# Token forms of the product-saving FFN units made in two portions, and S5 input loads split over two DMA queues

## The chip, the cores and the metric

The kernel runs on one core of a Trainium2 chip. The metric is the device time of one execution in microseconds (us); the median of a few runs is compared. Five engines work side by side, each through its own queue of instructions in a fixed order: TensorE (PE, the matmuls; PEld are its weight loads), VectorE (DVE), ScalarE (ACT), GpSimd (POOL) and SyncE (SP, which here only issues DMAs). ACT and POOL can issue DMAs too; such an instruction then stands in that engine's own queue.

## The reference, cut to what matters

The reference is one inference step of a two-layer decoder trunk for 512 prompt tokens and 8 sample tokens, all in float32. Layer 0 mixes with GLA and RG-LRU, layer 1 with S5 and HGRN2; each layer ends in a SwiGLU FFN. Two places matter here:

```python
def swiglu(h, w_in, w_out):
    gate, up = jnp.split(jnp.einsum('bld,df->blf', h, w_in), 2, axis=-1)
    return jnp.einsum('blf,fd->bld', jax.nn.silu(gate) * up, w_out)
...
    u, q, f, i, g = split_cols(z, ODD_SPLITS)
    y, s_re_new, s_im_new = s5_ssm(u, s_re, s_im, lam_re, lam_im, log_dt, b_re, b_im,
                                   c_re, c_im, d_skip)
```

## The kernel before, in words

Activations lie with the features on the partitions: a tile is 128 x 8 x 2 x 260, that is 8 groups of 128 features (index k) and two halves (hf) of 256 prompt and 4 sample tokens. A float32 product is made from three float32r products: each operand is split into a high part (`hhi`, a cast by ACT) and a low part (`hlo`, the rest, a subtraction by DVE), and high x high, low x high and high x low are added (`mm3`, L277 to L288). Weights are loaded as float32 by SP (`raw`, 3 buffers) and split in the same way (`whi`/`wlo`, 3 pairs, L242 to L243; `wxh`/`wxl` are more such tiles). One unit is 128 output features for all tokens: 48 matmuls.

`first_units` (L870) runs the first five units of a stage half by half, so that they can begin when the layer norm has done the first token half. A unit's result stands in `acc` (PSUM, two buffers) until an engine has taken it out: for a gate unit ACT (`sg`, Silu), for an up unit DVE (L1002, `sg` = acc x sg), followed by the split into `ah`/`al`.

**The FFN of layer 1** (`ffn`, L885): its first half (hb = 0) has 12 plain units (`fins`; the first five through `first_units`, L1010, the other seven in the loop at L1011), and then five units through `sw_unit` (L934). Such a unit makes a gate and an up block together from 2 x 2 blocks of weights and tokens with 7 block products in place of 8 (84 matmuls in place of 96). It needs sums of weight blocks (made by DVE in `raw`, L171 to L174) and four sums of token blocks, the token forms t1 to t4, which `t_forms` (L899) makes once. With b11, b12 the lower feature groups (k = 0 to 3) of the two token halves and b21, b22 the upper ones: t1 = b12 - b11, t2 = b22 - t1, t4 = b21 - t2 and t3 = b22 - b12. `join` adds high and low part again (DVE), `parts` splits a form (a cast by ACT, a subtraction by DVE); both go over two k at a time (128 x 520 elements). t1, t2 and t4 have tiles of their own. t3 is written over b12 in `hhi`/`hlo`, so it must wait until no plain unit reads these any more. The temporaries q1, q2, q3 come from the tag `t2k` with 6 buffers, as do `sg` and `p5`. In the program text the call stands behind all 12 plain units, at high priority (L1021 to L1022).

**The S5 input** (`odd_mixer`, L1802): the first four units of the layer-1 input projection make u. Each is written to DRAM (`Ud`, L1830, by SP; the sample tokens to `Usd`, L1850) and read back with another layout into `u8` (L1851 to L1854): eight loads of 128 KB each in rows of 256 bytes, and two small ones with rows of 32 bytes (L1853 into columns 0 to 7, L1854 into columns 73 to 80). All ten are issued by SP in that order. `s5_in` (L1861) multiplies columns 0 to 71 of `u8` (L1871). The trace shows `u8` as `u`.

What sets the order: the program text gives each instruction a place and a priority (`high_priority(offset=...)` moves it ahead by that much), and a planner, with durations that it assumes, then writes the queue of every engine. On the chip each engine takes its queue strictly in that order and waits where an input isn't there yet.

Of the kernel before, what the change touches and what calls it, by code (L numbers as in the profile page):

```python
# [33 lines left out]
HIGH = 3000  # L34
# [6 lines left out]
def build(tc, I, O):  # L41
    nc = tc.nc
    V, S, G, T, SY = nc.vector, nc.scalar, nc.gpsimd, nc.tensor, nc.sync
    with ExitStack() as ctx:
# [19 lines left out]
        def acc_tile():  # L64
            return ps["A"].tile([128, 2, 512], F32, tag="acc", name="acc")
# [4 lines left out]
        def t2k(nm):  # L70
            return tmp.tile([128, 2, HN], F32, tag="t2k", name=nm)
# [41 lines left out]
        def add(out, a, b):  # L113
            tt(out, a, b, ALU.add)
# [38 lines left out]
        LO, UP = slice(0, 4), slice(4, 8)  # L153
# [195 lines left out]
        h = (lambda k: hhi[:, k], lambda k: hlo[:, k])  # L349
# [74 lines left out]
        with tc.tile_pool(name="st", bufs=1, reuse_waits="tile") as st:  # L424
# [34 lines left out]
            for nm, ap in (  # L459
# [12 lines left out]
                n = ap.shape[0]  # L472
# [388 lines left out]
        def mmh(outs, wl_, a, ks, hf):  # L861
            ah, al = a
            ks = list(ks)
            for n, k in enumerate(ks):
                for out, (wh, wl) in zip(outs, wl_):
                    T.matmul(out, wh[:, k, :], ah(k)[:, hf, :], start=n == 0, stop=False)  # L866
                    T.matmul(out, wl[:, k, :], ah(k)[:, hf, :], start=False, stop=False)  # L867
                    T.matmul(out, wh[:, k, :], al(k)[:, hf, :], start=False, stop=n == len(ks) - 1)  # L868

        def first_units(us, alloc):  # L870
            ws.mark((3, 4), alloc)
            ws.off = FIRST
            wsl = [w() for w, _ in us]
            ws.off = HIGH
            for hf in range(2):
                for i in range(0, len(us), 2):
                    acc = acc_tile()
                    pair = list(enumerate(us))[i:i + 2]
                    mmh([acc[:, n - i, :HN] for n, _ in pair], [wsl[n] for n, _ in pair], h, range(8), hf)
                    for n, (_, ev) in pair:  # L880
                        ev(acc[:, n - i:n - i + 1, :HN], slice(hf, hf + 1))
# [3 lines left out]
        def ffn(l, mid=None):  # L885
            with tc.tile_pool(name=f"ff{l}", bufs=1, reuse_waits="tile") as fp:
# [8 lines left out]
                tf = []  # L895
# [3 lines left out]
                def t_forms():  # L899
                    swp = swx.enter_context(tc.tile_pool(name="sw", bufs=1, reuse_waits="tile"))  # L900
                    t1, t2, t4 = [tuple(swp.tile([128, 4, HN], F32R, name=f"t{n}{c}") for c in "hl") for n in (1, 2, 4)]
                    bq = lambda kq, hf: (hhi[:, kq, hf], hlo[:, kq, hf])

                    def join(out, kq, hf):
                        a_, b_ = bq(kq, hf)
                        add(out, a_.bitcast(F32), b_.bitcast(F32))

                    def parts(t, ks, src):
                        S.copy(t[0][:, ks], src)
                        sub(t[1][:, ks], src, t[0][:, ks].bitcast(F32))  # L910

                    t3 = bq(LO, 1)
                    qs = [(slice(q, q + 2), slice(q + 4, q + 6)) for q in (0, 2)]
                    for lo, up in qs:
                        q1, q2, q3 = t2k("q1"), t2k("q2"), t2k("q3")
                        join(q3, lo, 1)
                        join(q1, lo, 0)
                        sub(q1, q3, q1)
                        parts(t1, lo, q1)
                        join(q2, up, 1)  # L920
                        sub(q2, q2, q1)
                        parts(t2, lo, q2)
                        join(q3, up, 0)
                        sub(q3, q3, q2)
                        parts(t4, lo, q3)
                    for lo, up in qs:
                        q2, q3 = t2k("q2"), t2k("q3")
                        join(q3, lo, 1)
                        join(q2, up, 1)
                        sub(q2, q2, q3)  # L930
                        parts(t3, lo, q2)
                    return t1, t2, t3, t4, bq(LO, 0), bq(UP, 0), bq(UP, 1)

                def sw_unit(f):  # L934
                    w1, w2, wu, wg = ws.get("sw", 128 * f)
# [43 lines left out]
                for hb in range(2):  # L979
                    f0 = 11 * hb  # L980
                    fins = []
                    for d in range(0, 11, 2):
                        if l and f0 + d >= SW0:
                            break
                        nj = min(2, 11 - d)
                        fins += [(0, d, j) for j in range(nj)] + [(1, d, j) for j in range(nj)]
                    sg = {}

                    def fin_w(up, d, j):
                        return ws.get("fin", DFF * up + 128 * (f0 + d), 0, j)  # L990

                    def fin_ev(up, d, j, acc, hs=BOTH):
                        m = d + j
                        if up == 0:
                            if hs.start == 0:
                                sg[m] = t2k("sg")
                            act(sg[m][:, hs], acc, AF.Silu)
                            if hb == 0 and hs.stop == 2 and 3 <= m <= 10:
                                affine(last["act"], [m - 3])
                        else:  # L1000
                            s_ = sg[m][:, hs]
                            mul(s_, acc, s_)  # L1002
                            split(ah[:, m, hs], al[:, m, hs], s_)
                            if hs.stop == 2:
                                sg.pop(m)

                    n0 = 0
                    if hb == 0:
                        n0 = 5
                        first_units([(lambda u=u: fin_w(*u), lambda acc, hs, u=u: fin_ev(*u, acc, hs)) for u in fins[:n0]], walloc)  # L1010
                    for u in fins[n0:]:  # L1011
                        w = fin_w(*u)
                        acc = acc_tile()
                        mm3(acc, w, h, range(8))
                        fin_ev(*u, acc[:, :, :HN])
                        if hb == 0 and mid is not None:
                            side = side or mid(fp)
                            next(side, None)
                    if l:
                        if hb == 0:  # L1020
                            with tc.high_priority(offset=HIGH):  # L1021
                                tf[:] = t_forms()  # L1022
                        pg.close()
                        with tc.tile_pool(name=f"pS{hb}", bufs=8, space=PSUM, reuse_waits="tile") as ps["S"]:
                            for f in range(max(SW0, f0), f0 + 11):
                                sw_unit(f)
                        pg.enter_context(psum(2, 4, f"g{hb}"))
                        if hb:
                            swx.close()
                    for _ in side or ():  # L1030
                        pass
                    if hb == 0:
                        gt1 = gate1(l, 5)
                    for mp in range(4 - 2 * hb):
                        accs = [acc_tile() for _ in range(2)]
                        for n, (k0, nk) in enumerate(((8, 3), (0, 8))):
                            for j in range(2):
                                w = ws.get("fout", 256 * mp, f0 + k0, j)
                                mm3(accs[j], w, a, range(k0, k0 + nk), n == 0, n == 1, koff=k0)
                        for j in range(2):  # L1040
                            m = 2 * mp + j
                            if hb == 0:
                                evac_a(m, accs[j], gt1)
                            else:
                                evac_y(m, accs[j], gt1)
# [756 lines left out]
        def odd_mixer():  # L1802
            with tc.tile_pool(name="od", bufs=1, reuse_waits="tile") as mp_:
# [9 lines left out]
                Ud = dr.tile([4, 128, 8, 64], F32, name="Ud")  # L1813
                Usd = dr.tile([4, 128, 8], F32, name="Usd")
                Yd = dr.tile([4, 128, 8, 64], F32, name="Yd")
                Ysd = dr.tile([4, 128, 8], F32, name="Ysd")
                u8 = mp_.tile([128, 32, 81], F32, tag="m10", name="u8", bufs=2)
# [29 lines left out]
                with after_ln():  # L1847
                    G.memset(u8, 0.0)
                    G.memset(X[:, :, 0:1], 0.0)
                SY.dma_start(Usd.rearrange("m p b -> p m b"), u_s)  # L1850
                for e in range(8):  # L1851
                    SY.dma_start(u8[e * 16:(e + 1) * 16, :, 8:72], Ud[:, :, 7 - e, :].rearrange("m (g h) n -> h (m g) n", h=16))
                SY.dma_start(u8[0:16, :, 0:8], Usd.rearrange("m (g h) b -> h (m g) b", h=16))  # L1853
                SY.dma_start(u8[112:128, :, 73:81], Usd.rearrange("m (g h) b -> h (m g) b", h=16))  # L1854

                rot, vr = m8t("rot", (2, 16, 64)), m8t("vr", (2, 16, 64))
# [317 lines left out]
```

## Time and profile before

| | us |
|---|---|
| three runs | 1386.72, 1392.66, 1393.13; median 1392.66 |
| the profiled execution | 1392.64 |
| its span, first to last instruction | 1390.9 |
| around the span | 1.74 |
| busy: PE, DVE, ACT, POOL | 1320.2, 866.3, 551.6, 191.4 |
| mean granted TensorE clock | 0.975 of full speed |

A row of the timeline has start, duration, engine, line, operation, output<-inputs, shape, count and, in brackets, the idle time of the engine before it with what ended it. A row of a windows view has a stretch, its length, the busy time of each engine with its instructions, the granted TensorE clock, the share of the DMA engines that was busy, and GB/s. Line L111 is a helper (every DVE add, subtract and multiply), so tiles tell there what is meant. Times are from the span's start.

### The profile page before, as it was taken

The page shows a single profiled execution, that of the slowest core. Times are in us where ns is not written, and L with a number is a line of the kernel's source. Part 1 is how long each engine was busy: PE and PEld are TensorE (multiplying, and loading weights), DVE is VectorE, ACT ScalarE, POOL GpSimd, SP SyncE. Part 2 cuts the span into 40 slices and gives each one's busy share as a digit, 9 for nine tenths or more (in the row PEclk, how much of TensorE's full clock was granted, in tenths as well). Part 3 has the DMA queues.
Part 4 walks back from the last instruction along what each step waited for, and adds up shares of the span by engine and source line. Part 5 has one row for each costly group of instructions (what it writes and reads, how often), then busy time and mean ns, then how long its engine had stood idle before and what let it go on. Part 6 is the DMA issues. An engine that isn't in the chain of part 4 may idle for free. (4 is left out here: it accounts for less than half of the span.)

```text
span 1390.9 us, 29577 instructions
## 1 busy us (share of the span) xinstructions
PE 1320.2 (95%) x12503; PEld 1252.0 (90%) x12503; DVE 866.3 (62%) x1946; ACT 551.6 (40%) x962; POOL 191.4 (14%) x215
## 2 busy tenths in 40 slices
PE   6899999999999999999998999999897999999996
PEld 4798988999998999998988989889897999999996
DVE  4777755787996233323592784476839743888565
ACT  3554535362333222222264223363534632565431
POOL 2200010340011100000160431013500000000013
PEclk9999999999999999999999999999998999999997
DMA  9633353423446743446458445532121234332311
GB/s 284 210 132 104 111 188 122 152 69 99 137 161 207 241 153 131 145 134 220 149 204 180 136 132 176 145 123 80 61 91 57 77 95 122 92 91 73 126 62 62
DMA packets 172190, 185.53 MB, mean 133 GB/s; under 512 B 18412, under 2 KB 151914, under 8 KB 171802
## 3 DMA queue, kind: packets, MB, share of 16 engines
q1 hardware_dynamic: 166074, 166.43, 38.2%
q0 software_dynamic: 5744, 17.08, 3.7%
q8 instruction: 98, 1.61, 0.5%
q14 instruction: 34, 0.28, 0.1%
q10 hardware_dynamic: 240, 0.13, 0.0%
HBM read 167.11 MB, written 15.36 MB: 131 GB/s over the span
## 5 line engine op out<-in xcount | busy, mean ns | idle before, releaser
L242 ACT CAST whi<-raw 128x1024 fp32r<-128x1024 f32 (+2 forms) x166 | 154.4, 936 | 405.0 <-PE acc L286 298.5
L111 DVE TENSOR_TENSOR wlo<-raw,whi 128x1024 fp32r<-128x1024 f32 (+2 forms) x214 | 212.2, 1001 | 164.3 <-ACT whi L242 146.3
L284 PE MATMUL acc<-hhi,whi 128*128 128x260 f32 x1424 | 296.1, 289 | 4.6 <-issue 1.8
L286 PE MATMUL acc<-hlo,whi 128*128 128x260 f32 x1424 | 293.6, 287 | 1.6 <-DVE hlo L111 1.6
L288 PE MATMUL acc<-hhi,wlo 128*128 128x260 f32 x1424 | 292.3, 286 | 0.0
L284 PEld LDWEIGHTS acc<-hhi,whi 128*128 128x128 f32 x1424 | 221.9, 190 | 17.1 <-issue 8.5
L286 PEld LDWEIGHTS acc<-hlo,whi 128*128 128x128 f32 x1424 | 222.2, 190 | 4.8 <-DVE hlo L111 2.2
L288 PEld LDWEIGHTS acc<-hhi,wlo 128*128 128x128 f32 x1424 | 222.2, 190 | 2.3 <-issue 1.7
L286 PE MATMUL acc<-al,whi 128*128 128x260 f32 x576 | 116.7, 284 | 2.8 <-DVE al L111 2.8
L284 PE MATMUL acc<-ah,whi 128*128 128x260 f32 x576 | 117.2, 285 | 0.9 <-DVE x L123 0.8
L288 PE MATMUL acc<-ah,wlo 128*128 128x260 f32 x576 | 116.5, 284 | 0.0
L284 PEld LDWEIGHTS acc<-ah,whi 128*128 128x128 f32 x576 | 88.7, 189 | 4.5 <-issue 2.5
L286 PEld LDWEIGHTS acc<-al,whi 128*128 128x128 f32 x576 | 89.3, 190 | 3.2 <-DVE al L111 3.0
L288 PEld LDWEIGHTS acc<-ah,wlo 128*128 128x128 f32 x576 | 89.4, 190 | 0.0
L111 DVE TENSOR_TENSOR smp<-acc,gt 128x8 f32<-128x8 f32 (+1 forms) x72 | 11.5, 159 | 119.5 <-PE acc L288 94.4
L866 PE MATMUL acc<-hhi,whi 128*128 128x260 f32 x208 | 59.9, 290 | 3.4 <-ACT hhi L824 3.4
L868 PE MATMUL acc<-hlo,whi 128*128 128x260 f32 x208 | 59.2, 292 | 2.1 <-DVE hlo L111 1.3
L111 DVE TENSOR_TENSOR wxl<-raw,wxh 128x512 fp32r<-128x512 f32 (+1 forms) x74 | 56.4, 778 | 5.7 <-ACT wxh L160 3.1
L867 PE MATMUL acc<-hhi,wlo 128*128 128x260 f32 x208 | 58.9, 286 | 0.0
L160 ACT CAST wxh<-raw 128x512 fp32r<-128x512 f32 x64 | 38.3, 619 | 29.1 <-PE sb L943 20.4
L111 DVE TENSOR_TENSOR sg<-acc,sg 128x520 f32<-128x520 f32 (+1 forms) x32 | 19.8, 628 | 46.4 <-PE acc L288 42.0
L942 PE MATMUL sb<-hhi,wxh 128*128 128x260 f32 x128 | 38.1, 298 | 7.0 <-DVE sb L111 7.0
(640 smaller groups left out, 2855.6 us busy)
## 6 DMA issues: line engine op xcount, KB each, us to landing
raw<-in_w_ada_dram SPq DMA_DIRECT2D x40, 1024.0 KB, 6.7
raw<-in_ffn_w_in_dram SPq DMA_DIRECT2D x26, 1024.0 KB, 5.1
raw<-in_ffn_w_in_dram SPq DMA_DIRECT2D x36, 512.0 KB, 4.7
raw<-in_ffn_w_out_dram SPq DMA_DIRECT2D x16, 1024.0 KB, 5.4
raw<-in_ev_w_in_dram SPq DMA_DIRECT2D x10, 1024.0 KB, 8.1
raw<-in_od_w_in_dram SPq DMA_DIRECT2D x10, 1024.0 KB, 5.6
raw<-in_w_ada_dram SPq DMA_DIRECT2D x16, 512.0 KB, 7.8
raw<-in_ffn_w_out_dram SPq DMA_DIRECT2D x16, 384.0 KB, 3.1
```

Source lines behind the costliest of these rows:

```text
L111: V.tensor_tensor(out=out, in0=a, in1=b, op=op)
L160: S.copy(t[0][:, q], src[:, q])
L242: S.copy(hi[:, :nk, :m], rj)
L284: T.matmul(acc[:, hf, :HN], wh[:, k - koff, :], ah(k)[:, hf, :], start=st, stop=False)
L286: T.matmul(acc[:, hf, :HN], wh[:, k - koff, :], al(k)[:, hf, :], start=False, stop=False)
L288: T.matmul(acc[:, hf, :HN], wl[:, k - koff, :], ah(k)[:, hf, :], start=False, stop=sp)
L866: T.matmul(out, wh[:, k, :], ah(k)[:, hf, :], start=n == 0, stop=False)
L867: T.matmul(out, wl[:, k, :], ah(k)[:, hf, :], start=False, stop=False)
L868: T.matmul(out, wh[:, k, :], al(k)[:, hf, :], start=False, stop=n == len(ks) - 1)
L942: T.matmul(out[:, 0], w[0][:, off + k], t[0][:, k], start=st and k == 0, stop=False, skip_group_check=True)
```

## The change

`t_forms` becomes a generator. Its first portion makes t1, t2 and t4 and is called directly behind `first_units`, at the same high priority; its second makes t3 and is called where all was made before. q1, q2 and q3 of the first portion are allocated once, ahead of the loop over the two pairs of k, and are used again by the second pass. The S5 loads are issued by SP and ACT in turn: ACT issues the small load L1853, now the first of the ten, and the four with odd e; SP issues the four with even e and then L1854.

```diff
                     qs = [(slice(q, q + 2), slice(q + 4, q + 6)) for q in (0, 2)]
+                    q1, q2, q3 = t2k("q1"), t2k("q2"), t2k("q3")
                     for lo, up in qs:
-                        q1, q2, q3 = t2k("q1"), t2k("q2"), t2k("q3")
                         join(q3, lo, 1)
...
                         parts(t4, lo, q3)
+                    yield t1, t2, t3, t4, bq(LO, 0), bq(UP, 0), bq(UP, 1)
                     for lo, up in qs:
                         q2, q3 = t2k("q2"), t2k("q3")
...
                         parts(t3, lo, q2)
-                    return t1, t2, t3, t4, bq(LO, 0), bq(UP, 0), bq(UP, 1)
...
                         first_units([(lambda u=u: fin_w(*u), lambda acc, hs, u=u: fin_ev(*u, acc, hs)) for u in fins[:n0]], walloc)
+                    if l and hb == 0:
+                        with tc.high_priority(offset=HIGH):
+                            tgen = t_forms()
+                            tf[:] = next(tgen)
                     for u in fins[n0:]:
...
                             with tc.high_priority(offset=HIGH):
-                                tf[:] = t_forms()
+                                next(tgen, None)
...
                 SY.dma_start(Usd.rearrange("m p b -> p m b"), u_s)
+                S.dma_start(u8[0:16, :, 0:8], Usd.rearrange("m (g h) b -> h (m g) b", h=16))
                 for e in range(8):
-                    SY.dma_start(u8[e * 16:(e + 1) * 16, :, 8:72], Ud[:, :, 7 - e, :].rearrange("m (g h) n -> h (m g) n", h=16))
-                SY.dma_start(u8[0:16, :, 0:8], Usd.rearrange("m (g h) b -> h (m g) b", h=16))
+                    (S if e % 2 else SY).dma_start(u8[e * 16:(e + 1) * 16, :, 8:72], Ud[:, :, 7 - e, :].rearrange("m (g h) n -> h (m g) n", h=16))
                 SY.dma_start(u8[112:128, :, 73:81], Usd.rearrange("m (g h) b -> h (m g) b", h=16))
```

## Rows read from the trace of the kernel before

**Rows 1.** The page's first part: busy time of each engine.

```profile
PE 1320.2 (95%) x12503; PEld 1252.0 (90%) x12503; DVE 866.3 (62%) x1946; ACT 551.6 (40%) x962; POOL 191.4 (14%) x215
```

**Rows 2.** What PE waited for, 1055 to 1080 us (total, times, longest).

```profile
PE sb L943 <- DVE wxl L111: 4.0, 1, 4.0
PE sb L942 <- DVE sb L111: 1.9, 1, 1.9
PE sb L942 <- DVE sg L111: 1.7, 1, 1.7
PE sb L944 <- DVE t1l L111: 1.4, 1, 1.4
```

**Rows 3.** Windows: the start of the `sw_unit`s, and plain units of equal length.

```profile
1055.00:1085.00 30.00, 21.00 (x137) 20.11 (x137) 25.99 (x44) 12.93 (x26) 0.00 (x0) 0.77 0.13 37
1005.00:1035.00 30.00, 30.00 (x252) 30.00 (x252) 9.04 (x12) 8.48 (x13) 0.00 (x0) 1.00 0.29 88
```

**Rows 4.** DVE groups, shapes apart, 1043 to 1078 us: busy, mean ns, idle before.

```profile
L111 DVE TENSOR_TENSOR q<-hhi,hlo 128x520 f32<-128x520 f32 x12 | 8.0, 691 | 0.0
...
L111 DVE TENSOR_TENSOR q<-q,q 128x520 f32<-128x520 f32 x8 | 5.5, 691 | 0.0
...
L111 DVE TENSOR_TENSOR t1l<-q,t1h 128x520 fp32r<-128x520 f32 x2 | 1.4, 691 | 0.0
```

**Rows 5.** DVE timeline: the first form instructions, and the last plain unit's evacuation.

```profile
1043.37 2.52 DVE L111 TENSOR_TENSOR q<-hhi,hlo 128x520 f32<-128x520 f32 x4
...
1059.55 0.69 DVE L111 TENSOR_TENSOR sg<-acc,sg 128x520 f32<-128x520 f32 x1
```

**Rows 6.** PE timeline: first matmuls of the sixth plain unit, last matmuls of the twelfth.

```profile
1018.06 0.40 PE L284 MATMUL acc<-hhi,whi 128*128 128x260 f32 x2
...
1058.19 0.40 PE L288 MATMUL acc<-hhi,wlo 128*128 128x260 f32 x2
```

**Rows 7.** Windows by DVE's load: plain units, and the end of them with the first `sw_unit`.

```profile
1005.00:1043.00 38.00, 38.00 (x319) 38.00 (x319) 12.35 (x16) 11.94 (x18) 0.00 (x0) 1.00 0.28 84
...
1053.00:1077.00 24.00, 15.00 (x103) 14.11 (x102) 23.96 (x41) 10.39 (x20) 0.00 (x0) 0.80 0.09 26
```

**Rows 8.** DVE timeline: layer norm's last instruction; evacuation of third and fourth unit, second half.

```profile
1004.92 0.42 DVE L817 TENSOR_TENSOR hlo<-h32h,hhi 128x256 fp32r<-128x256 f32 x1 [1.32 <-ACT hhi L79]
...
1015.47 0.76 DVE L111 TENSOR_TENSOR sg<-acc,sg 128x260 f32<-128x260 f32 x2 [2.71 <-PE acc L868]
```

**Rows 9.** PE timeline: end of a unit in `odd_mixer`; around the wait for `u`.

```profile
749.62 0.40 PE L288 MATMUL acc<-hhi,wlo 128*128 128x260 f32 x2
...
759.49 0.40 PE L286 MATMUL acc<-hlo,whi 128*128 128x260 f32 x2
765.10 3.17 PE L1871 MATMUL mx<-u,bt 128*64 128x72 f32 x48 [5.21 <-DMA u<-Ud]
```

**Rows 10.** SP's queue in time: the ten loads into `u8`.

```profile
751.30 6.65 SPq L1852 DMA_DIRECT2D u<-Ud  x8
757.99 1.14 SPq L1853 DMA_DIRECT2D u<-Usd  x1
759.18 1.82 SPq L1854 DMA_DIRECT2D u<-Usd  x1
```

**Rows 11.** L1853: us from issue to landing.

```profile
DMA to landing us min/median/max: 6.7/6.7/6.7
```

**Rows 12.** Windows: before the loads, during them, behind them.

```profile
745.00:750.00 5.00, 5.00 (x45) 5.00 (x44) 0.00 (x0) 0.13 (x1) 0.00 (x0) 1.00 1.02 338
751.00:763.00 12.00, 8.89 (x74) 8.68 (x73) 3.47 (x6) 7.66 (x11) 0.00 (x0) 1.00 1.21 105
765.00:770.00 5.00, 4.90 (x56) 4.79 (x57) 2.70 (x10) 0.00 (x0) 1.42 (x2) 0.50 0.59 188
```

**Rows 13.** ACT timeline while the loads are issued: the first and last of six rows.

```profile
749.87 1.05 ACT L242 CAST whi<-raw 128x1024 fp32r<-128x1024 f32 x1 [5.28 <-PE acc L286]
...
757.10 2.94 ACT L79 ACTIVATE x<-x,ba,ga 128x520 f32<-128x520 f32 x4
```

## The prediction, made before the changed kernel was run

> **What bounds the kernel now.** I read the page's busy times first: PE works 1320.2 of 1390.9 us [rows 1], so only what makes PE wait, or slows it, can pay. I then asked what PE waited for in the two stretches that the diff touches. When the `sw_unit`s begin, PE stops four times within 25 us, 9.0 us in all, and each time DVE is named [rows 2]. The windows give the full loss there, waits and the lower clock behind them together: 137 matmuls in 30 us, where plain units have 252 in 30 us, 0.119 us each [rows 3]. 115 are missing: 115 x 0.119 = 13.7 us, at a mean granted clock of 0.77 against 1.00. DVE's load explains it: from 1053 to 1077 it is busy 23.96 of 24 us, while over the plain units just before it has 12.35 of 38 us [rows 7]. The second stretch is the S5 input: PE stands 5.2 us for `u` [rows 9], and the granted clock is 0.50 (that is 1.2 GHz) from 765 to 770 us [rows 12].
>
> The sum is made against the profiled execution, 1392.64 us (1390.9 of span and 1.74 around it); the median shown is 1392.66, so nothing is to be corrected.
>
> **What is moved off DVE.** All four forms are 28 DVE instructions: 12 joins and 8 subtractions [rows 4], and 8 low parts, of which the t1l row is one of four alike, two instructions each. t1, t2 and t4 have 20 of the 28 (8 joins, 6 subtractions, 6 low parts). One costs 2.52 / 4 = 0.63 us of DVE time when they follow one another [rows 5]. So 12.6 us leave the crowded stretch, and 8 instructions, 5.0 us, stay. Six casts go with them on ACT, which is busy 11.94 of 38 us where they arrive [rows 7]: I cost these at nothing, the cover being ACT's 26 idle us.
>
> Without the 12.6 us, DVE has half of its work in those 24, and three of the four waits lose their ground: t1l is long done, and wxl and sb stood behind forms in DVE's queue. What stays of 13.7 us:
> - The first product needs the PSUM buffer that the last plain unit leaves. That unit's matmuls end at 1058.19 + 0.40 = 1058.6 [rows 6]; its evacuation starts only at 1059.55 and takes 0.69 us [rows 5]. With DVE free it starts at once, and 0.8 us of the 1.7 [rows 2] remain.
> - t3 and the second unit's weights still meet there. Bounds: 0, and the 1.9 us that PE waited for sb [rows 2]; the nearest row says crowding, now half of what it was, so I take 1.0.
>
> Gain: 13.7 - 0.8 - 1.0 = 11.9 us.
>
> **What it costs where it goes.** In the plain units DVE has 38 - 12.35 = 25.6 us idle [rows 7] for 12.6 us of forms. The layer norm's last low part ends at 1004.92 + 0.42 = 1005.3 [rows 8], so the forms can run from there; back to back they hold DVE to 1017.9, and one weight split falls due between them (1.2 us): 1019.1. Queued behind them is the evacuation of the third and fourth unit, ready at 1015.47 and 0.76 us long [rows 8]; the sixth unit needs their buffer at 1018.06 [rows 6]. In the worst order it ends at 1019.9, 1.8 us late; with an order that takes the evacuation first, 0. I take 0.5. If the idle time weren't there, the full 12.6 us would come back as waits. The low parts of the weights of later units are also behind the forms, but each is made a unit, 5.7 us, ahead of its use. The temporaries: three of six buffers are held to 1019, when at most three `sg` live; the next `sg` is needed only when the sixth unit ends, at 1018.06 + 48 x 0.119 = 1023.8. Nothing.
>
> **The S5 loads.** Before, SP issues ten loads from 751.30 to 761.0 [rows 10]. The last one that `s5_in` needs, L1853, is issued at 757.99 and lands 6.7 us later [rows 11], at 764.7; PE starts at 765.10 [rows 9]. From SP's side alone, five loads instead of ten should be issued in half the time, 4.9 us earlier. But while the loads run the DMA engines are busy more than fully (share 1.21) at 105 GB/s, where the megabyte before them, in longer rows, moved at 338 GB/s [rows 12]. That is a DMA limit and not a queue waiting to issue; and I read the 6.65 / 8 = 0.83 us of one issue [rows 10] as SP held up by it. Then two queues share the same engines, and all ten end when they end now. Bounds: 0, and 4.9 us of the wait with the slow clock behind it. The slow stretch has some 4.9 us of PE work at half speed, so 2.4 us: 7.3 us. I take 0.2, since the busy share is the nearest row. The Trainium skill says the same in "DMA: Bandwidth & Descriptors", section "Issuing engines are not separate DMA queues": starting DMAs from several engines saves only the issuing time. The trace agrees in the share of 1.21; by the rule alone the sum would be the same within 0.2 us.
>
> ACT's five issues come at about 0.83 us, 4.2 us, in a stretch where it has six rows from 749.87 to 760.04 [rows 13]. Behind them stand evacuations that PE needs for the next unit; but whatever PE loses there it would have lost waiting for `u` until 765, so I cost it at nothing as long as `u` is what ends last.
>
> **Sum.** -11.9 + 0.5 - 0.2 = -11.6 us: 1392.64 - 11.6 = 1381 us. A measurement of this kernel tells a change from none at about 0.5%, 7.0 us; the forecast is over it by 4.6 us.
>
> **The rivals.**
> 1. *DVE stays the bound (0.20).* The `sw_unit`'s weights are a chain too: DVE sums in `raw`, an ACT cast, a DVE low part, and the longest wait, 4.0 us, names wxl [rows 2]. If that chain ends last without the forms also, the wxl and sb waits (5.9 us) stay. 1381 + 5.9 = 1387. For it: the rows name wxl and not a form. Against it: these wxl stood in a queue filled with forms; half of 24 us was theirs.
> 2. *Two queues are faster (0.15).* If the loads are held up by the one ring and not by the DMA engines, the S5 bound holds: 1381 - 7.1 = 1374. For it: a share above 1 shows that several packets overlap in an engine, so more rings may overlap more. Against it: 105 GB/s over 12 us without a gap.
> 3. *The planner moves the S5 products ahead (0.06), slower.* The queue of PE is written from assumed times: it has the first product of `u` at 759.9, 5.2 us before `u` is there [rows 9]. If the planner believes that two queues halve the loading, it puts that product before both units that run from 749.7 to 759.9. On the chip ACT issues its five loads only behind its casts and scalings, from 760.0 [rows 13]; 760.0 + 4.2 + 6.7 [rows 11] = 770.9. PE then waits from 749.7 to 770.9, 21.2 us instead of 5.2: +16.0. That gives 1381 + 16 = 1397. It decides the sign once this wait exceeds 5.2 + 11.4 = 16.6 us. For it: the plan is wrong by 5.2 us already. Against it: both errors must come together; if only the first does, it costs at most the 10.2 us of the two units, and the total is about 1391.
> 4. *The change does not do what it says (0.05).* The planner could leave the forms where they run now: they start at 1043.37 [rows 5] although their inputs are there at 1005. Then 1392. Against it: they start 15 us ahead of their place in the program text, and that place now lies some 40 us earlier.
>
> **How the numbers follow.** The forecast has 0.54. With both costs at their lower bounds it gives 1392.6 - 12.9 - 0.2 = 1379.5, at their upper ones 1392.6 - 11.0 + 1.8 = 1383.4. The range must also take in rivals 1 and 2: 1374 to 1390; outside are rivals 3 and 4 and the mild form of 3. *Faster by over 0.5%* (below 1385.7): nearly all of the forecast (0.50), rival 2 (0.15) and a little of rival 1 (0.02): 0.67. *Slower by over 0.5%*: rival 3 and orders that I haven't seen, 0.07. The rest, 0.26, is within 0.5%.
>
> **What would show it.** Right: the q, t1, t2 and t4 instructions on DVE lie between 1004 and 1020; the t1l and wxl waits of rows 2 are gone; a 30 us window from the end of the plain units holds over 225 matmuls at a clock above 0.95; the plain units still run without a wait over 1 us. For S5: `u` lands within 1 us of 765 and PE waits about 5 us. Wrong: DVE still over 90% busy behind the plain units with PE waiting for wxl (rival 1); a wait for `u` under 2 us (rival 2), or one that begins at 750 (rival 3); forms still at 1043 (rival 4). I would be wrong in the main step if PE lost new time between 1005 and 1055, where now it loses nothing.

## The result and the profile after

The changed kernel takes 1380.74 us (median of 15 runs, 1375.76 to 1387.70), the kernel before 1392.69 us (15 runs, 1386.45 to 1396.83). The ratio is 0.9915, 95% interval 0.9897 to 0.9934: some 12 us faster, 9 to 14 by the interval. The forecast was 1381.0 us. The profiled execution of the changed kernel is one of its quicker ones: 1376.92 us, with a span of 1375.2 us. A comparison of the two profiled spans therefore shows 15.7 us where the medians differ by 12; where the rest lies is said in the last section.

The page's first part, changed kernel; the instruction counts are those of [rows 1]:

```profile
PE 1313.4 (96%) x12503; PEld 1244.8 (91%) x12503; DVE 866.6 (63%) x1946; ACT 552.3 (40%) x962; POOL 193.1 (14%) x215
```

No work has left any engine. DVE is as busy as before, so what changed is when it is busy. What PE waited for from 1055 to 1080 us, changed kernel (total, times, longest):

```profile
PE sb L942 <- DVE sg L111: 1.2, 1, 1.2
PE sb L942 <- DVE sb L111: 0.7, 1, 0.7
```

Of the four waits of [rows 2], the ones for wxl (4.0 us) and t1l (1.4 us) are gone, and the other two are shorter: 9.0 us have become 1.9. The windows that answer to [rows 3] and [rows 7] (columns as there: busy time and count of PE, PEld, DVE, ACT, POOL, then granted clock, DMA share, GB/s):

```profile
1055.00:1085.00 30.00, 27.61 (x226) 26.98 (x224) 24.73 (x44) 17.68 (x37) 0.00 (x0) 1.00 0.25 74
1005.00:1035.00 30.00, 30.00 (x253) 30.00 (x252) 20.92 (x30) 13.79 (x21) 0.00 (x0) 1.00 0.35 106
1053.00:1077.00 24.00, 22.07 (x182) 21.65 (x181) 18.95 (x34) 12.78 (x28) 0.00 (x0) 1.00 0.30 88
1005.00:1043.00 38.00, 38.00 (x319) 38.00 (x318) 24.94 (x36) 16.05 (x24) 0.00 (x0) 1.00 0.29 89
```

In the first row PE does 226 matmuls where it did 137, and the granted clock is 1.00 where it was 0.77. In the third, DVE has fallen from 23.96 to 18.95 of 24 us. In the last, it has risen from 12.35 to 24.94 of 38 us, by 12.6 us. That this is the very figure of the forms is chance: three of the 20 form instructions ran before 1005 us, and most of t3's four joins, which stood behind the window before [rows 5], now lie in it. PE lost nothing there: 319 matmuls in 38 us, as before.

The DVE timeline of the changed kernel says where the forms now are:

```profile
1002.16 1.30 DVE L111 TENSOR_TENSOR q<-hhi,hlo 128x520 f32<-128x520 f32 x2
...
1012.98 0.77 DVE L111 TENSOR_TENSOR sg<-acc,sg 128x260 f32<-128x260 f32 x2
...
1020.04 0.70 DVE L111 TENSOR_TENSOR t4l<-q,t4h 128x520 fp32r<-128x520 f32 x1
...
1040.94 2.52 DVE L111 TENSOR_TENSOR q<-hhi,hlo 128x520 f32<-128x520 f32 x4
...
1056.01 0.69 DVE L111 TENSOR_TENSOR wxl<-raw,wxh 128x512 fp32r<-128x512 f32 x1
1056.61 0.69 DVE L111 TENSOR_TENSOR sg<-acc,sg 128x520 f32<-128x520 f32 x1
```

t1, t2 and t4 are made from 1002.16 to 1020.7. The evacuation of the third and fourth unit stands in the middle of them, at 1012.98, with no idle time noted before it. Of the forms only t3 comes later; its joins start at 1040.94. The last plain unit is evacuated at 1056.61. Now the PE timeline, changed kernel: the last plain unit's end, the first `sw_unit` product, and the first product behind this block of `sw_unit`s:

```profile
1055.76 0.40 PE L288 MATMUL acc<-hhi,wlo 128*128 128x260 f32 x2
1057.36 0.39 PE L942 MATMUL sb<-hhi,whi 128*128 128x260 f32 x1 [1.20 <-DVE sg L111]
...
1110.62 0.40 PE L284 MATMUL acc<-ah,whi 128*128 128x260 f32 x2
```

The last of these rows, in the kernel before:

```profile
1124.50 0.40 PE L284 MATMUL acc<-ah,whi 128*128 128x260 f32 x2
```

This isolates the stage from all that lies ahead of it. From the end of the last plain unit to the first product behind the block, it took 1124.50 - 1058.59 [rows 6] = 65.9 us, and takes 1110.62 - 1056.16 = 54.5 us. The stage gives 11.4 us, all but the whole of the result.

The same two rows can be read in the traces of all the kernels below. The stage takes 54.5 us in each of the nine traces with early forms and no work added, and 64.6 to 66.4 us in the five others. Three of these five have the forms as before (65.9, 64.6 and 64.8 us); against them it gives 10.1 to 11.4 us.

**The S5 input.** Views of the changed kernel. PE's timeline, around the place where it waited for `u` [rows 9]:

```profile
758.89 0.80 PE L284 MATMUL acc<-hhi,whi 128*128 128x260 f32 x2 [2.85 <-ACT sf L79]
...
766.05 1.77 PE L1875 MATMUL mx<-u,bt 128*64 128x72 f32 x48
```

SP's queue, as in [rows 10]:

```profile
751.19 1.93 SPq L1857 DMA_DIRECT2D u<-Ud  x4
```

ACT's timeline; its queue's own rows are named ACTq:

```profile
755.06 3.13 ACTq L1857 DMA_DIRECT2D u<-Ud  x2
758.24 0.60 ACT L79 ACTIVATE sf<-acc 128x520 f32<-128x520 f32 x1 [4.72 <-DMA u<-Ud]
```

ACT's four issues of `Ud` loads together (least, middle and longest duration in ns, first and last start), and the last of them alone:

```profile
L1857 ACTq DMA_DIRECT2D u<-Ud x4: 309/322/511, 750.9 to 757.9; - x4
...
757.88 0.31 ACTq L1857 DMA_DIRECT2D u<-Ud  x1
```

And the windows of [rows 12], with the slow stretch:

```profile
751.00:763.00 12.00, 9.15 (x61) 8.95 (x61) 2.73 (x6) 5.81 (x8) 0.00 (x0) 0.79 1.36 103
765.00:770.00 5.00, 5.00 (x76) 4.78 (x75) 2.68 (x10) 1.66 (x3) 1.43 (x2) 1.00 0.95 313
760.00:765.00 5.00, 5.00 (x26) 5.00 (x26) 1.26 (x2) 5.00 (x8) 0.00 (x0) 0.52 0.95 51
```

The loading in two parts; and its first part in the kernel before:

```profile
753.00:762.00 9.00, 6.15 (x40) 5.95 (x39) 2.38 (x5) 4.28 (x7) 0.00 (x0) 0.78 1.51 94
762.00:765.00 3.00, 3.00 (x17) 3.00 (x16) 1.23 (x1) 3.00 (x5) 0.00 (x0) 0.53 0.54 29
```

```profile
753.00:762.00 9.00, 6.89 (x58) 6.68 (x56) 1.47 (x3) 5.66 (x8) 0.00 (x0) 1.00 1.43 108
```

SP is through its four loads in 1.93 us; the loads still move 103 GB/s (105 before), and the first S5 product starts at 766.05 (765.10 before): the second queue brought `u` no sooner. The wait has another name. ACT stood idle for 4.72 us around its last two issues, the evacuation `sf` behind them started only at 758.24, and PE stood 2.85 us for it.

The issuing itself took little of that: the 3.13 us are the time from the start of one issue (755.06) to the end of the next (757.88 + 0.31), and one issue took 0.31 us. The rest is a wait in front of each. The DMAs of SP and ACT tell of their landing through eight semaphores (counters that instructions wait on), used in turn, and the trace shows an issue wait until the DMA that used its semaphore before has landed. For the issue at 755.06 that was a load of other weights, issued by SP at 744.95 and landed at 755.04; for the one at 757.88 it was SP's first load of `u`, landed at 757.86. In all eight traces with two queues these two issues start 0.02 to 0.03 us behind such a landing. The load issued last lands at 765.37; from 762 to 765 us the DMA share is 0.54 only.

The half clock (0.52) now falls on plain matmuls at 760 us instead of on S5 products at 765 us.

### The profile page after: what moved, and what is told of

Its sections match the earlier page's. It is cut to its first block, busy times and chain, and to the rows that moved or that the text cites. A ratio compares the mean times of both kernels' runs of the same rounds, so it can differ in the third digit from the quotient of the medians.

```text
span 1375.2 us, 29578 instructions
## 1 busy us (share of the span) xinstructions
PE 1313.4 (96%) x12503; PEld 1244.8 (91%) x12503; DVE 866.6 (63%) x1946; ACT 552.3 (40%) x962; POOL 193.1 (14%) x215
## 5 line engine op out<-in xcount | busy, mean ns | idle before, releaser
L575 POOL TENSOR_TENSOR s<-x 128x520 f32<-128x520 f32 x4 | 6.9, 1720 | 277.0 <-DVE x L111 254.2
```

## The experiments

Differences are against the changed kernel or the kernel before, as each says; ratios are against the kernel before, measured beside them.

**Each part alone.** The forms early, the loads as before:

```diff
-S.dma_start(u8[0:16, :, 0:8], Usd...)
 for e in range(8):
-    (S if e % 2 else SY).dma_start(u8[e * 16:(e + 1) * 16, :, 8:72], ...)
+    SY.dma_start(u8[e * 16:(e + 1) * 16, :, 8:72], ...)
+SY.dma_start(u8[0:16, :, 0:8], Usd...)
```

> The forms made early as in the changed kernel, the S5 loads all on SP in the old order. Theory (the forms carry the gain, the loads next to nothing): 11.4 us under the kernel before, some 1381; the sw start as in the changed kernel (230 matmuls or more in 1050 to 1080 us), and at the S5 input the old wait for u of some 5 us, no wait for sf. Rival (the second queue carries several us of the 12): 5 to 7 us under the kernel before.

1380.34 us, ratio 0.9929 (0.9902 to 0.9955). In its trace, what PE waited for at the S5 input, and the window of the `sw_unit`s' start:

```profile
PE mx L1875 <- DMA u<-Ud: 4.7, 1, 4.7
```

```profile
1050.00:1080.00 30.00, 28.07 (x232) 27.65 (x231) 22.77 (x39) 16.22 (x31) 0.00 (x0) 1.00 0.29 85
```

The forms alone give the whole gain. The kernel before with the S5 loads of the change (the same lines the other way round):

> The kernel before with the two-queue S5 loads alone. By the prediction: 0.2 us under the kernel before, so no difference that can be measured. By the trace of the changed kernel (last Qs evacuation 1.9 us earlier, from the same start): 1.9 us under it. Rival 2 (two queues faster): 7 us under. Of the profile: a wait for sf near 758 us and none for u if the trace of the changed kernel repeats; the loads land at 764 to 766 us in every case where the DMA engines bound them.

1392.51 us, ratio 1.0021 (1.0001 to 1.0042): no gain, neither the 0.2 us of the prediction nor the 1.9 us that the changed kernel's trace let expect. PE's waits there are like those of the changed kernel:

```profile
PE acc L284 <- ACT sf L79: 2.9, 1, 2.9
PE mx L1871 <- DMA u<-Ud: 0.7, 1, 0.7
```

Rival 2 (two queues faster, 7 us) is out.

**What the order of the loads is worth.** All on SP, the small one first (in the kernel before, L1853 moved ahead of L1851; in SP's queue it then stood second, at 750.11 us, behind one load of `Ud`):

> All ten loads on SP as before, but the small load of Usd issued first instead of ninth. If the last of the needed loads sets the end by its place in the issue order: u is complete some 0.8 us earlier (one issue less ahead of the last needed one), PE's wait for u about 4.4 us, the time 0 to 1.1 us lower. If the total transfer sets it: wait 5.2 us, time unchanged. Any gain over 1.5 us would mean that order, and not the second queue, is what the S5 part changed.

1392.06 us, ratio 1.0029 (1.0008 to 1.0051). PE stands 5.0 us at the S5 input, and its first S5 product follows SP's first load by 14.0 us (749.67 to 763.7), against 13.8 in the kernel before. The order within the queue does nothing that shows. The kernel before had a median of 1390.27 us beside this kernel, S5 alone, forms-only and the later products, against 1392.69 us in the first comparison; I read no loss out of 1.0029, nor out of the 1.0021 of S5 alone.

**Half of the loads**, to see whether the loading goes with the rows moved, and what the wait is worth. Only the even ones of the eight loads of `Ud` are issued; the other rows of `u8` keep their zeros, so S5 computes with half of its input:

```diff
-for e in range(8):
+for e in range(0, 8, 2):
     SY.dma_start(u8[e * 16:(e + 1) * 16, :, 8:72], ...)
```

> The forms as changed, the loads all on SP, and only the four loads of even e of the eight (the odd rows of u stay zero, so S5's results differ). It prices the wait for u. If the loading time goes with the rows loaded: u is there some 5 to 6 us earlier, near 759 us, the wait of 4.7 us and the slow clock behind it go, and the time is 5 to 7 us under the forms-only kernel, some 1374. If the wait is hidden by what follows (another wait behind it takes its place): 0 to 2 us under it, 1379 to 1380.

1377.71 us, ratio 0.9914 (0.9893 to 0.9935); against the forms-only kernel's 0.9929 that is 0.0015, 2 us, with intervals that overlap widely. Three views: SP's queue, PE's first S5 product, and PE's waits from 740 to 775 us.

```profile
754.98 1.93 SPq L1856 DMA_DIRECT2D u<-Ud  x4
```

```profile
763.24 1.75 PE L1875 MATMUL mx<-u,bt 128*64 128x72 f32 x48 [2.76 <-DMA u<-Usd]
```

```profile
PE mx L1875 <- DMA u<-Usd: 2.8, 1, 2.8
PE mx L1875 <- DMA bt<-BATd: 1.2, 1, 1.2
```

The first product now comes 763.24 - 754.98 = 8.3 us after the first load, instead of 14; the wait ends with the small load, fifth in the queue. The time goes with the rows moved, or with the number of loads, which was halved with them. Yet PE still waits 4.0 us. With fewer loads the planner put the S5 products earlier in PE's queue: the first 48 matmuls of S5 stand 26 plain matmuls further ahead (26 x 0.119 = 3.1 us), so PE reaches them sooner and waits again, and later `bt` is late. Most of the 6 us is taken back at once.

**Later products.** The forms-only kernel with the first eight of S5's sixteen pairs asked for behind the next plain unit instead of around it:

```diff
-s5_in(0, 4)
 unit("in", 1280, 0, ...)
 affine(last["act"], range(4, 8))
-s5_in(4, 4)
 unit("in", 1280, 1, ...)
+s5_in(0, 4)
+s5_in(4, 4)
 s5_in(8, 4)
```

> Forms early, loads all on SP as before, and the S5 products asked for one plain unit (5.7 us) later in the program. Theory (u is there at about 765, and all that PE lacks is work that does not need it): the wait for u of 5.2 us falls to 0 or 1 and the slow clock behind it goes, so 5 to 7 us under the forms-only kernel, some 1375. Rival (the planner already places the products where it likes, whatever the place in the program; or the time comes back as a later wait for what the S5 products feed): the same as the forms-only kernel within 1 us.

1380.30 us, ratio 0.9925 (0.9901 to 0.9950), the same as forms-only. My theory failed here. The wait and the window behind it:

```profile
PE mx L1875 <- DMA u<-Ud: 3.5, 1, 3.5
```

```profile
765.00:770.00 5.00, 5.00 (x69) 4.86 (x70) 2.91 (x11) 0.00 (x0) 1.61 (x3) 0.50 0.58 180
```

3.5 us instead of 4.7, with the half clock behind it. In PE's written order the first products stand only 16 matmuls later (16 x 0.119 = 1.9 us), and not a whole unit: the planner places them by its own times, whatever their place in the text. Why it found nothing else to put there was not tried.

**Is it DVE's time?** The changed kernel with 20 joins more behind t3's portion, into scratch that nothing reads:

```diff
         parts(t3, lo, q2)
+    for lo, up in qs:
+        q2 = t2k("q2")
+        for _ in range(10):
+            join(q2, lo, 1)
```

> The changed kernel with 20 extra joins on DVE (20 x 0.61 = 12.2 us) behind t3's portion, into scratch that nothing reads. Theory (DVE time at the sw start is what the waits were made of): most of the gain goes, 8 to 12 us over the changed kernel, 1389 to 1393, with waits for DVE back in 1050 to 1080 us. Rival (the waits were made of t1, t2, t4 and t3 being late as inputs, and not of DVE's time): under 2 us over the changed kernel.

1389.97 us, ratio 0.9998 (0.9980 to 1.0016): the whole gain is gone, though t1, t2 and t4 are made as early as in the changed kernel. PE's waits from 1060 to 1090 us, and the window:

```profile
PE sb L947 <- DVE wxl L111: 4.1, 2, 3.8
PE sb L946 <- DVE sg L111: 2.4, 1, 2.4
PE sb L946 <- DVE sb L111: 1.9, 2, 1.1
PE sb L946 <- ACT wxh L160: 1.3, 1, 1.3
```

```profile
1060.00:1090.00 30.00, 20.13 (x143) 18.58 (x142) 29.97 (x52) 11.34 (x23) 0.00 (x0) 0.89 0.14 43
```

DVE is busy 29.97 of 30 us, and the wait for wxl is back, 3.8 us against the 4.0 of [rows 2]. Work that nobody needs made it. So it was DVE's time and not the forms as late inputs.

**Is it the place?** The changed kernel with the first portion called behind the eleventh plain unit instead of the fifth; everything else of the change stays:

```diff
-if l and hb == 0:
-    with tc.high_priority(offset=HIGH):
-        tgen = t_forms()
-        tf[:] = next(tgen)
 for u in fins[n0:]:
     ...
     fin_ev(*u, acc[:, :, :HN])
+    if l and hb == 0 and u is fins[10]:
+        with tc.high_priority(offset=HIGH):
+            tgen = t_forms()
+            tf[:] = next(tgen)
```

> The changed kernel with the first portion of the forms behind the eleventh plain unit instead of the fifth, about 34 us later; the split of t3 and the single set of temporaries stay as changed. Theory (the gain is the 12.6 us of DVE work leaving the crowded stretch): the forms run between about 1040 and 1062 us, the waits come back, 8 to 12 us over the changed kernel, some 1390. Rival (the splitting of t3 or the one set of temporaries carries it, not the place): the same as the changed kernel within 2 us.

1391.82 us, ratio 0.9996 (0.9976 to 1.0015). The window from 1053 to 1083 us and its longest waits:

```profile
1053.00:1083.00 30.00, 21.82 (x136) 20.01 (x137) 24.60 (x42) 13.13 (x27) 0.00 (x0) 0.77 0.24 70
```

```profile
PE sb L942 <- ACT t1h L909: 2.1, 1, 2.1
PE sb L942 <- ACT t2h L909: 2.0, 1, 2.0
PE sb L942 <- DVE sb L111: 1.5, 1, 1.5
```

136 matmuls at 0.77, almost the row of the kernel before (137 at 0.77), with other names: here the forms themselves are what is late. The split of t3 and the one set of temporaries carry nothing. With the eighth unit in place of the eleventh (`fins[7]`):

> The changed kernel with the first portion behind the eighth plain unit instead of the fifth. Theory (any place will do that leaves 12.6 us of idle DVE time before the sw units, and DVE is idle two thirds of the plain units): the forms run from about 1024 to 1045 us, no wait comes back, within 2 us of the changed kernel. Rival (the place directly behind the first units matters): 3 us or more over it.

1380.23 us, ratio 0.9930 (0.9910 to 0.9950). The forms run on DVE from 1018.29 to 1045.0, and PE's waits and count at the start of the `sw_unit`s are those of the changed kernel, as the window shows:

```profile
1055.00:1085.00 30.00, 28.07 (x232) 27.65 (x231) 24.95 (x45) 18.09 (x38) 0.00 (x0) 1.00 0.24 71
```

Directly behind the first five units is not special; of the three places tried, the two ahead of the crowd give the same gain.

**The temporaries.** The changed kernel with the three buffers taken anew in each half:

```diff
-q1, q2, q3 = t2k("q1"), t2k("q2"), t2k("q3")
 for lo, up in qs:
+    q1, q2, q3 = t2k("q1"), t2k("q2"), t2k("q3")
     join(q3, lo, 1)
```

> The changed kernel with the three temporaries taken anew for each half, six buffers instead of three. By the prediction (the buffers cost nothing either way): the same as the changed kernel within 2 us, 1381. Rival (one set makes the second half wait for the first, or two sets keep sg from its buffer): 1 to 3 us in either direction, with a wait in the plain units between 1005 and 1035 us in the second case.

1375.13 us, ratio 0.9887 (0.9859 to 0.9915), but of four runs only. Its trace has the same two waits at the `sw_unit`s (1.2 and 0.7 us) and the same 253 and 232 matmuls in the two stretches, and nothing in it that could be 5 us quicker. Hence once more, beside the changed kernel itself:

> The changed kernel itself, beside the next two on the same chip. Theory: 11 to 12 us under the kernel before, 0.9915 of it; its first S5 product 13.5 to 15 us after SP's first load of u.

> The changed kernel with six temporaries instead of three, again, since four runs gave 1375.1 us. Theory (its trace has the same waits and the same 253 and 232 matmuls in the two stretches, so nothing in it can be 5 us faster): within 2 us of the changed kernel beside it. Rival (two sets are faster): 4 to 6 us under the changed kernel beside it.

The changed kernel gave 1380.98 us, ratio 0.9945 (0.9921 to 0.9970); two sets gave 1379.03 us, 0.9934 (0.9914 to 0.9954). The low figure did not come again. Two sets with all loads on SP:

> Forms early with six temporaries, and the S5 loads all on SP in the old order. If neither the buffers nor the second queue are worth anything: within 2 us of the changed kernel beside it. If the second queue only costs (S5 alone was measured at 1.0021 of the kernel before): 1 to 3 us under it.

1380.66 us, ratio 0.9943 (0.9919 to 0.9967). Apart from those four runs, no version with early forms can be told from another; none is shown to beat the changed kernel.

**The S5 loads side by side.** From SP's first load of `u` to the first S5 product, PE's waits ahead of it (for sf and for u), and the stretch from the start of the unit ahead to the last evacuation of `Qs`, each from the kernel's own trace:

```
kernel                queues  first load  product    us   waits sf + u  stretch
before                SP          751.30   765.10  13.8     0  + 5.2     54.1
forms only            SP          754.27   768.6   14.3     0  + 4.7     52.9
small load first      SP          749.67   763.7   14.0     0  + 5.0     52.9
two sets, SP          SP          751.81   766.5   14.7     0  + 5.0     53.0
changed               SP, ACT     751.19   766.05  14.9    2.8 + 0       52.2
S5 alone              SP, ACT     751.54   766.2   14.7    2.9 + 0.7     51.9
changed, again        SP, ACT     750.94   766.3   15.4    3.0 + 0.8     52.1
forms late            SP, ACT     751.26   765.5   14.2    2.9 + 1.9     51.7
forms at 8th unit     SP, ACT     750.76   764.8   14.0    2.9 + 1.8     51.4
```

One queue or two, the first product comes 14 to 15 us after the first load. (In the first profile of the changed kernel PE does not wait for `u`; its last load lands at 765.37, 14.2 us after the first issue.) The stretch is shorter with two, 51.9 against 53.2 us in the mean, with no overlap. The traces that are not in the table fit: 13.8 to 14.6 us and stretches of 51.4 to 52.1 us in the three others with two queues, 14.5 and 52.6 us with the later products on SP. But from there to the first `sw_unit` product the two profiles of the changed kernel alone differ by 4 us (260.9 and 264.9), and the times of S5 alone show no gain. Whether those 1.3 us reach the end stays open.

## Why the prediction was right

The time was right (1381.0 against 1380.74) and so was the reason for nearly all of it. That the two agree to 0.3 us is luck: the measured gain is known only as 9 to 14 us, and terms that were off by 0.2 to 0.5 us cancel. By its steps:

- **The loss of 13.7 us, and the 12.6 us of DVE work that leaves.** Shown. The plain units took the forms without a loss to PE, the stage shrank by 11.4 us (10.1 at the least), and putting 12.2 us of useless work back, or the forms back to their old time, took the whole gain away (ratios 0.9998 and 0.9996).
- **0.8 us that stays for sg.** It was 1.2. I let the evacuation start at the unit's end; DVE was still at a wxl part begun at 1056.01, so it started at 1056.61, 0.45 us after the end at 1056.16.
- **1.0 us for t3 and the second unit's weights.** 0.7 us, the wait for sb. The two together were 1.9 against 1.8, the gain 11.4 against 11.9. The sign that I named, over 225 matmuls above 0.95 in 30 us from the end of the plain units, was missed by little: from 1056.16 on there are 224, at 1.00 (the window with 226 starts 1.2 us ahead of that end).
- **0.5 us in the plain units.** It was 0. The forms started 3 us earlier than I had allowed, at 1002.16 among the layer norm's last low parts; the evacuation at 1012.98 stands between them and not behind them, and 253 matmuls run in the 30 us. DVE took less than its idle time, and the place behind the eighth unit did as well as the one behind the fifth.
- **The S5 loads, 0.2 us.** The total shows none. The reason given, that the DMA engines and not the queue bound them, holds for most of the loading: 14 to 15 us either way, 8.3 us for half of the rows, and from 753 to 762 us a DMA share of 1.51 with two queues and 1.43 with one. It does not hold for the end: from 762 to 765 us the share is 0.54, and what is left is mostly the load that ACT could issue only at 757.88. How soon `u` would be there with two queues and without that hold, no run shows. The Trainium skill's rule in "DMA: Bandwidth & Descriptors", section "Issuing engines are not separate DMA queues", is that starting DMAs from several engines saves only the time of issuing them. The 14 to 15 us either way agree with that.
- **ACT's issues at no cost while `u` ends last.** This step was wrong as a picture. I added up 4.2 us of issuing, 0.83 us each, and hid it behind `u`. In fact ACT's five issues took 0.31 to 0.51 us each, 2.0 us together. What the sum did not have is that an issue waits for an earlier landing: ACT stood 4.72 us before `sf`, some 4.1 of them for that, and PE waited 2.6 to 3.3 us for `sf` in every trace with two queues. It cost nothing in sum only because the wait for `u` became as much shorter.

Of the rivals, 1 (wxl ends last without the forms too) is out: no wait for wxl is left. 2 is out by the S5 part alone. The sign that I gave for it, a wait for `u` under 2 us, did come (none, and 0.8 us in the second profile); it was a bad sign, for PE had spent that time in the wait for `sf`. 3 did not come with two queues, where the first products stand two matmuls later than before; but its mechanism is real, since with half of the loads the planner did move the products ahead and PE waited for what it had not foreseen. 4 is out by the DVE timeline.

## What to carry to other kernels

When an engine that is 62% busy on average makes the bounding engine wait, look at the stretch: the work to move is what has early inputs and late users, and it may go to any idle time ahead of the crowd, as the fifth and eighth unit gave the same and the eleventh nothing. A wait's named releaser need not be the culprit: wxl was named, the forms ahead of it in the queue were to blame, and idle work in their place brought the same name back. Before spreading loads over a second queue, compare the GB/s and the DMA share during them, and ask what stands behind the issues in the second engine's own queue, and which earlier landing each issue has to wait for.

## What was not expected of the hardware

- **A DMA issue can hold a compute engine without being long itself.** ACT's issues took 0.31 to 0.51 us each, but two of them first waited for an earlier DMA with the same semaphore to land (one of them for SP's first load of `u`, at 757.86 us), and the evacuation behind them started after 4.72 us of idle time.
- **An issue grew long from the fifth in one queue on.** SP issued its four loads of `u` in 1.93 to 1.99 us, 0.48 us each, in every kernel where it had only four. Where more stood in a row in its queue, the fifth took 1.1 to 3.1 us; eight loads took it 6.65 us in the kernel before [rows 10]. With two queues seven issues began within 2 us, and none took over 0.72 us.
- **The same code runs at another clock from run to run.** From 800 to 890 us, which the change does not touch, the granted clock was 1.00 in the changed kernel's first profile and 0.94 in the kernel before and in the changed kernel's second. From the last evacuation of `Qs` to the first product of `y5h` the first profile took 95.7 us (796.5 to 892.2), and the kernel before 99.9 us (798.1 to 898.0). The second profile of the changed kernel took 100.2 us there (796.7 to 896.9), with a span of 1379.0 us. Most of these 4.2 us were lost again: from 890 to 970 us the clock was 0.91 in the first profile and 0.98 in the kernel before, and at the end of the last plain unit the first profile is 2.4 us ahead (1056.16 against 1058.59). So the 15.7 us are these 2.4, the stage's 11.4 and some 1.8 behind it.
- **Fewer bytes gave little time.** Half of the loads brought the first S5 product 6 us closer to the first load (8.3 us against 14.3 in the forms-only kernel) and the total some 2 us, if any.
